# A loop of 200 matmuls without a reader behind the last product of an AdaLoRA linear layer

## Chip, cores and metric

The kernel runs on one core of a Trainium2 chip. The metric is the device time of one execution in microseconds. The kernel before takes 162.21 us (median of 3 runs, 161.91 to 162.54).

## What is computed

A linear layer with a low-rank addition whose rank directions are scaled. There are 16 x 2048 = 32,768 rows of 256 inputs, 256 outputs, and rank 16, all in float32:

```python
x_flat = x.reshape(-1, in_dim)            # 32768 x 256
y = x_flat @ W                            # 256 x 256
lora_out = x_flat @ lora_A                # 256 x 16
lora_out = lora_out * lora_E
lora_out = lora_out @ lora_B              # 16 x 256
y = y + scale * lora_out
```

The input is 33.5 MB and the output the same, so 67 MB pass between HBM and SBUF.

## The kernel before

**Folding.** The low-rank part is folded into the weights once: `weff = W + (lora_A * lora_E * scale) @ lora_B`, in bf16 (L158 to L176). After that the kernel is one product, `x @ weff`.

**Tiling.** The rows are cut into six pieces (`PLAN`: 48, 32, 48, 32, 48, 48 rows for each of the 128 partitions). A piece lives in one of four SBUF slots named `xy`, and its outputs overwrite its inputs there. A piece is worked through in steps of 8 rows per partition (`S = 8`), 32 steps in all (`NS`).

**One step on each engine.**

- VectorE rounds 8 x 256 inputs to bf16 (`rounded`, L151, into `xb`) and later copies the transposed step out of PSUM (`copied`, L155, from `ps_xt` to `xt`).
- TensorE transposes a step with 8 matmuls against the identity (`transposed`, L190; two bf16 travel as one float32 word) and multiplies a step with 16 matmuls (`multiplied`, L201): the weights loaded into the array are a 128x128 slice of `xt`, the moving operand is half of `weff` (128x256), and the result goes to `ps_y`.
- ScalarE copies each half of a product from `ps_y` into the slot (L224).
- SP, the queue of the loads and stores, issues the store of a piece when its last copy is done (L104, called from L236), and the two late loads.

**Order on TensorE.** Its work is a hardware loop of 16 passes (L211), each with two steps, transposing one step ahead: pass by pass `transposed(1)`, `multiplied(0)`, `transposed(0)`, `multiplied(1)`. Double buffers (index `k`, 0 or 1) hold `xb`, `xt` and `ps_xt`. The last `transposed(0)` transposes a step that does not exist, and its result is not read. The loop's control on TensorE's sequencer is an ALU_OP and a COMPARE_BRANCH at the end of each pass, and one MOVE ahead of it.

**Signals.** TensorE raises `s_t` after each transposed step (VectorE waits for it, and SP for two of its issues) and `s_m` after each half product (ScalarE waits for it). ScalarE returns the buffers of `ps_y` over `can_y`. Behind the loop TensorE has only four waits that reset semaphores (L117 three times, L250). At the very end SP waits until every store has landed (L251, L252).

Of the kernel before, what the change touches and what calls it, by code (L numbers as in the profile page):

```python
# [12 lines left out]
HOLD = 14, 1  # L13

ISSUE_LOAD, ISSUE_STORE = {5: 16}, {3: 26}

S, G = 8, 4
P = 128
# [17 lines left out]
def kernel(tc, x, W, lora_A, lora_B, lora_E, scale, out):  # L36
    nc = tc.nc
# [17 lines left out]
    def sbuf(name, shape, dt):  # L55
        return nc.alloc_sbuf_tensor(name, shape, dt).ap()

    def psum(name, shape, dt):
        return nc.alloc_psum_tensor(name, shape, dt).ap()
# [8 lines left out]
    weff = sbuf("weff", [P, KC, M], BF16)  # L68
# [6 lines left out]
    pairs = [t[:, :, :].rearrange("p s t -> p (s t)").bitcast(BF16).rearrange("p (s t c) -> p s t c", s=S, c=KC) for t in xt]  # L75
    ps_xt = [psum(f"psum_xt{k}", [P, S, P], FP32) for k in range(2)]
# [42 lines left out]
    def take(sem):  # L119
        nc.tensor.wait_ge(sem, 1).then_inc(sem, -1)  # L120
# [66 lines left out]
    def transposed(k):  # L187
        nc.tensor.wait_ge(can_t[k], 1)
        for j in range(S):
            done = nc.tensor.transpose(ps_xt[k][:, j, :], words[k][:, j, :], ident)  # L190
            if j == 1:
                done.then_inc(can_t[k], -1)
        done.then_inc(s_t.sem, 1)

    def multiplied(k):
        take(can_m)
        for h in range(S // G):
            nc.tensor.wait_ge(can_y[h][k], 1)
            for j in range(G):
                for c in range(KC):  # L200
                    done = nc.tensor.matmul(  # L201
                        ps_y[h][:, j, :], pairs[k][:, h * G + j, :, c], weff[:, c, :],
                        start=(c == 0), stop=(c == KC - 1))
                if j == 0:
                    done.then_inc(can_y[h][k], -1)
            done.then_inc(s_m.sem, 1)
# [4 lines left out]
    with nc.tensor.Fori(0, NS // 2):  # L211
        for k in range(2):
            transposed(1 - k)
            multiplied(k)
    s_t.total, s_m.total = NS + 1, NS * S // G

    for h in range(S // G):
# [2 lines left out]
    for i, r in [(i, r + g) for i, r in steps for g in range(0, S, G)]:  # L220
        n += 1
        nc.scalar.wait_ge(s_m.sem, n)
        t, h = divmod(n - 1, S // G)
# [64 lines left out]
```

## Time and profile before

| what | value |
|---|---|
| profiled execution, time | 162.07 us |
| its span, first to last instruction | 160.7 us |
| mean granted TensorE clock | 0.829 of full speed |
| TensorE matmuls: busy, share of the span, count | 92.6 us, 58%, 780 |
| TensorE weight loads | 83.6 us, 52%, 780 |
| VectorE | 76.7 us, 48% |
| ScalarE | 63.2 us, 39% |
| moved by DMA | 67.42 MB, mean 419 GB/s |

The span counts from the first to the last instruction; 1.37 us of the execution lie outside it. A matmul's duration runs from its start to the modelled end of its result and overlaps the next matmul's, so a pace is read from starts or from merged pieces, not from a mean duration. In lists of groups, `PEld` is the weight load and `PEldq` or `PEq` the sequencer of TensorE; the `xN` is a count.

### The profile page before, as it was taken

To read this page: it belongs to the slowest core of one execution; us is meant where nothing else is said; L and a number is where in the kernel's file an instruction comes from. 1 tells how busy PE (TensorE), PEld (TensorE's weight loads), DVE (VectorE), ACT (ScalarE), POOL (GpSimd) and SP (SyncE) were. 2 spreads that over 40 slices of the span, in tenths; PEclk is the share of its full clock that TensorE was granted. 3 is DMA by queue.
4 is the path that set the end of the run, shared out by engine and by line. 5 is a ranking of instruction groups with operands and counts; after the bars stand their busy time and mean duration, and the time that the engine had idled before them with its cause. 6 is when DMAs were issued, how large, how long until landed. Compare 5 with 4: busy or idle time off the path is not lost.

```text
span 160.7 us, 1867 instructions
## 1 busy us (share of the span) xinstructions
PE 92.6 (58%) x780; PEld 83.6 (52%) x780; DVE 76.7 (48%) x67; ACT 63.2 (39%) x65; POOL 0.7 (0%) x6
## 2 busy tenths in 40 slices
PE   0258099999999200000299999999999980000000
PEld 0047089999999100000279999999999970000000
DVE  0173396989894000000585989898989510000000
ACT  0303118686777400000026686867777681000000
POOL 0100000000000000000000000000000000000000
PEclk9999959999999965555559999999999999555555
DMA  6999998999999999999999999999999999999994
GB/s 195 420 477 416 400 489 383 446 422 428 432 473 310 504 453 416 400 424 416 501 428 428 404 416 489 428 418 404 428 436 416 432 481 404 428 489 416 428 404 196
DMA packets 2370, 67.42 MB, mean 419 GB/s; under 512 B 432, under 2 KB 448, under 8 KB 576
## 3 DMA queue, kind: packets, MB, share of 16 engines
q1 hardware_dynamic: 2160, 67.37, 98.0%
q10 hardware_dynamic: 208, 0.03, 0.1%
q14 instruction: 2, 0.02, 0.0%
HBM read 33.85 MB, written 33.55 MB: 419 GB/s over the span
## 4 chain that ended last, share of the span: by engine, by line
PE 48%; DMA 30%; ACT 2%; DVE 2%; SPq 1%; issue 0%
PE psum_y L201 31%; DMA out_dram<-xy 20%; PE psum_xt L190 17%; DMA xy<-in_x_dram 11%; ACT xy L224 2%; DVE xb L151 2%; SPq L104 1%
## 5 line engine op out<-in xcount | busy, mean ns | idle before, releaser
L224 ACT COPY xy<-psum_y 128x1024 f32<-128x1024 f32 x64 | 61.9, 1017 | 64.8 <-PE psum_y L201 64.8
L201 PE MATMUL psum_y<-weff,xt 128*128 128x256 bf16 x512 | 63.8, 280 | 0.0
L190 PE MATMUL psum_xt<-ident,xb 128*128 128x128 f32 x264 | 37.6, 291 | 32.3 <-DVE xb L151 32.3
L201 PEld LDWEIGHTS psum_y<-weff,xt 128*128 128x128 bf16 x512 | 51.5, 101 | 6.8
L151 DVE CAST xb<-xy 128x2048 bf16<-128x2048 f32 x32 | 38.9, 1218 | 32.9 <-DMA out_dram<-xy 27.7
L190 PEld LDWEIGHTS psum_xt<-ident,xb 128*128 128x128 f32 x264 | 32.9, 151 | 33.8 <-DVE xb L151 33.4
L155 DVE COPY xt<-psum_xt 128x1024 f32<-128x1024 f32 x32 | 39.2, 1224 | 11.7 <-PE psum_xt L190 11.7
L163 PE MATMUL psum_xt<-ident,a_sb 128*16 128x128 f32 x2 | 0.6, 394 | 5.9 <-POOL ident L137 5.9
L224 ACT ACT_TABLE_LOAD x1 | 1.3, 1283 | 5.2 <-PEq L133 5.2
L163 PEld LDWEIGHTS psum_xt<-ident,a_sb 128*16 128x16 f32 x2 | 0.1, 90 | 5.9 <-issue 5.9
L159 DVE CAST b_bf<-b_sb 16x256 bf16<-16x256 f32 x1 | 0.3, 280 | 5.4 <-DMA b_sb<-in_lora_B_dram 5.4
L172 PE MATMUL psum_xt<-b_bf,ate 16*128 16x256 bf16 x2 | 0.6, 400 | 1.2 <-DVE ate L167 1.2
L167 DVE TENSOR_SCALAR ate<-psum_xt,e_sb 16x256 bf16<-16x256 f32 x1 | 0.5, 472 | 1.6 <-DMA e_sb<-in_lora_E_dram 1.6
L176 DVE TENSOR_TENSOR weff<-w_sb,psum_xt 128x512 bf16<-128x512 f32 x1 | 0.7, 689 | 0.8 <-PE psum_xt L172 0.8
L172 PEld LDWEIGHTS psum_xt<-b_bf,ate 16*128 16x128 bf16 x2 | 0.1, 108 | 1.7 <-DVE ate L167 1.7
L137 POOL TENSOR_SCALAR_AFFINE_SELECT ident<-ident 128x128 f32<-128x128 f32 x1 | 0.3, 298 | 0.2 <-POOL ident L135 0.2
L135 POOL MEMSET ident<- 128x128 f32 x1 | 0.2, 205 | 4.6 <-POOLq L133 4.6
L269 POOL MEMSET const-bfloat16-1.0<- 128x1 bf16 x1 | 0.1, 102 | 0.0
L269 POOL MEMSET const-uint8-127<- 128x1 uint8 x1 | 0.1, 102 | 0.0
L269 POOL MEMSET const-float32-0.0<- 128x1 f32 x1 | 0.1, 99 | 0.2 <-issue 0.2
L269 POOL MEMSET const-float32-1.0<- 128x1 f32 x1 | 0.1, 99 | 0.0
## 6 DMA issues: line engine op xcount, KB each, us to landing
out_dram<-xy SPq DMA_DIRECT2D x4, 6144.0 KB, 29.5
xy<-in_x_dram SPq DMA_DIRECT2D x3, 4096.0 KB, 26.4
xy<-in_x_dram SPq DMA_DIRECT2D x2, 6144.0 KB, 22.6
out_dram<-xy SPq DMA_DIRECT2D x2, 4096.0 KB, 25.4
xy<-in_x_dram SPq DMA_DIRECT2D x2, 3072.0 KB, 36.5
xy<-in_x_dram SPq DMA_DIRECT2D x1, 2048.0 KB, 7.9
w_sb<-in_W_dram SPq DMA_DIRECT2D x1, 256.0 KB, 2.7
a_sb<-in_lora_A_dram ACTq DMA_DIRECT2D x1, 16.0 KB, 2.8
```

Source lines behind the costliest of these rows:

```text
L104: ins = queue.dma_start(**aps)
L137: s_id.by(nc.gpsimd.affine_select(out=ident, in_=ident, compare_op=mybir.AluOpType.not_equal, fill=1.0, base=0, pattern=[[-1, P]], channel ...
L151: nc.vector.tensor_copy(out=xb[t % 2], in_=slot(i)[:, r:r + S, :]).then_inc(can_t[t % 2], 1)
L155: nc.vector.tensor_copy(out=xt[t % 2], in_=ps_xt[t % 2]).then_inc(can_m, 1)
L163: at_done = nc.tensor.transpose(ps_at[:, c, :], a_sb[:, c, :], ident)
L167: s_v.by(nc.vector.tensor_scalar(out=ate, in0=ps_at, scalar1=e_sb, scalar2=float(scale), op0=mybir.AluOpType.mult, op1=mybir.AluOpType.mult))
L172: aeb_done = nc.tensor.matmul(ps_aeb[:, c, :], ate[:, c, :], b_bf, start=True, stop=True)
L176: s_v.by(nc.vector.tensor_add(out=weff, in0=w_sb, in1=ps_aeb))
L190: done = nc.tensor.transpose(ps_xt[k][:, j, :], words[k][:, j, :], ident)
L201: done = nc.tensor.matmul(ps_y[h][:, j, :], pairs[k][:, h * G + j, :, c], weff[:, c, :], start=(c == 0), stop=(c == KC - 1))
L224: y = nc.scalar.copy(out=slot(i)[:, r:r + G, :], in_=ps_y[h])
L269: nc = _bacc.Bacc("TRN2", target_bir_lowering=False, num_devices=1)
```

## The change

One constant, and a second hardware loop on TensorE behind the first. It has 25 passes of 8 matmuls. The weights are slices of `xt1`, the transposed inputs of the last step, and the moving operand is the first half of `weff`. Every matmul writes the same 128x256 float32 part of `ps_xt[0]`, each with `start` and `stop` set, so none adds to another's result. No semaphore is touched, and nothing reads that part again.

```diff
 ISSUE_LOAD, ISSUE_STORE = {5: 16}, {3: 26}
+
+SPARE = 25, 8
...
         for k in range(2):
             transposed(1 - k)
             multiplied(k)
+    with nc.tensor.Fori(0, SPARE[0]):
+        for j in range(SPARE[1]):
+            nc.tensor.matmul(
+                ps_xt[0][:, :2, :].rearrange("p s t -> p (s t)"), pairs[1][:, j, :, 0], weff[:, 0, :],
+                start=True, stop=True)
     s_t.total, s_m.total = NS + 1, NS * S // G
```

## Prediction

> **What bounds the kernel now.** I read the strips of the page first, then the chain of waits in order of time, then stretches of time, then single lines. The strips show 40 slices of 4.02 us each:
>
> ```profile
> PE   0258099999999200000299999999999980000000
> ACT  0303118686777400000026686867777681000000
> PEclk9999959999999965555559999999999999555555
> DMA  6999998999999999999999999999999999999994
> ```
>
> The transfers run at nine tenths or more in nearly every slice. TensorE works in two long blocks, and in the last seven slices (28 us) neither TensorE nor ScalarE does anything: the kernel only drains its last store. The granted TensorE clock falls to half some slices after TensorE goes quiet. So the change puts its work where TensorE is idle and the end is set elsewhere. The end of the chain of waits, in order of time (start us, length us, what), says by what:
>
> ```profile
> 76 pieces in order of time: start us, us, what
> ...
> 127.77 1.75 PE psum_y L201 x16
> 129.51 0.87 PE psum_xt L190 x8
> 130.39 0.89 PE psum_y L201 x8
> 131.27 0.02 issue
> 131.30 0.90 ACT xy L224
> 132.20 0.01 issue
> 132.21 1.02 ACT xy L224
> ```
>
> The last matmuls feed two ScalarE copies that end at 132.21 + 1.02 = 133.23. Behind them SP issues the store of the last piece (48 rows per partition, 6144 KB). The timeline has that issue at 133.25 us, and the span ends at 160.7: the last 27.5 us are that store and what is still queued ahead of it. Stretches of time show the same, and at what rate (columns: us, busy time of each engine, granted clock, DMA share, GB/s):
>
> ```profile
> 20.00:53.00 33.00, 32.93 (x286) 30.28 (x287) 26.98 (x24) 21.73 (x23) 0.00 (x0) 0.95 1.03 434
> 55.00:78.00 23.00, 0.00 (x0) 0.00 (x0) 0.00 (x0) 0.00 (x0) 0.00 (x0) 0.56 0.98 422
> 86.00:131.00 45.00, 45.00 (x415) 41.86 (x414) 37.71 (x32) 32.80 (x34) 0.00 (x0) 1.00 1.00 430
> 133.00:154.00 21.00, 0.00 (x0) 0.00 (x0) 0.00 (x0) 0.22 (x1) 0.00 (x0) 0.58 1.02 440
> ```
>
> With TensorE busy the transfers moved 434 and 430 GB/s, with TensorE idle 422 and 440. Last, the loop control of the existing TensorE loop (L211) and the products (L201), with duration in ns as min/median/max and the first and last start in us:
>
> ```profile
> L211 PEldq ALU_OP  x16: 36/36/42, 21.4 to 130.7; - x16
> L211 PEldq COMPARE_BRANCH  x16: 76/208/217, 21.5 to 130.8; - x16
> L211 PEldq MOVE  x1: 33/33/33, 10.4 to 10.4; - x1
> ```
>
> ```profile
> L201 PEld LDWEIGHTS psum_y<-weff,xt x512: 96/98/152, 13.7 to 131.8; 128*128 128x128 bf16 x171
> L201 PE MATMUL psum_y<-weff,xt x512: 269/273/421, 13.7 to 131.9; 128*128 128x256 bf16 x171
> ```
>
> The sequencer took its last ALU_OP at 130.7 while the last product started at 131.9. It runs 1.2 us, some 11 matmuls, ahead of the array.
>
> **The change, part by part.** It removes nothing, moves nothing, issues no DMA and adds no semaphore wait. It adds one MOVE and 25 passes of 8 weight loads, 8 matmuls, one ALU_OP and one COMPARE_BRANCH, on TensorE's queue alone.
>
> *The array's time.* Each added matmul has the form of L201's: the same weight slice (128x128 bf16 out of xt1), the same moving operand weff, 256 columns. The 273 ns in the row is one matmul from start to finish and overlaps the next, so I take the pace from the chain. Its L201 pieces start at 85.85 and again at 130.39, 17 halves of 24 matmuls later: 44.54 us / 408 = 109 ns. The weight load (98 ns) fits under that, as it does in L201. So 200 x 0.109 = 21.8 us. The first can start one pace behind the last product, at 131.9 + 0.1 = 132.0. The last ends at 132.0 + 199 x 0.109 + 0.27 = 154.0 us.
>
> *The clock.* That pace needs the full grant. It is 1.00 from 86 to 131, and in the stretch after the last product the records drop to half only at 136.4, over 4 us after TensorE fell quiet. The added matmuls come without a gap, so I take 1.00. At half clock the chain has 16 products in 3.41 us (from 81.27), 213 ns each. That is the other end: 200 x 0.213 = 42.6 us.
>
> *Loop control.* A taken branch costs the sequencer about 0.31 us from the start of the ALU_OP to the end of the branch (0.1 + 0.208). One pass gives the array 8 x 0.109 = 0.87 us of work, so the sequencer has 0.56 us left for 16 instructions, 35 ns each. How fast it issues is shown by L201's second half: those 8 products wait for the ScalarE copy that ends at 130.61 (timeline: the pair of copies from 128.68 takes 1.93), and the ALU_OP behind them runs at 130.68. Sixteen instructions went in 0.07 us, 4 ns each. So a pass needs some 0.38 us of sequencer against 0.87 us of array, and branches hide under the matmuls. The existing loop agrees: 45.00 of 45.00 us busy over eight or nine branches. The slow bound comes from the transposes behind a branch: 16 instructions within the 0.70 us from the branch's end (125.75) to the next semaphore instruction (126.45), though that one also waits for VectorE. It gives 0.31 + 0.70 = 1.01 us per pass, 25.3 us in all, end at 157.5. I take 0.87.
>
> *Behind the loop* TensorE has four semaphore instructions (L117 x3, L250), 0.15 us apart in the records. At most 0.6 us, so TensorE is done between 154.0 and 154.6. Nobody waits for it: no later instruction reads ps_xt[0], and the signals that ScalarE and SP need (s_m, s_t) are raised by the old loop.
>
> *Code.* The page has two instruction packets in the whole run (0.02 MB). If the longer program needs one more first-time fetch, the nearest rows are the small loads at the start, 2.8 us (lora_A) and 5.5 us (lora_E) to landing. Even 5.5 moves TensorE's end only to 160.1.
>
> [...]
>
> *The transfers.* The matmuls read SBUF while the last store does. Rates by stretch bound this from both sides: 440 to 430 GB/s would lengthen 21 us by 0.5 us; 422 to 434 would shorten it by 0.6 us. The two idle stretches differ more from each other than from the busy ones, so I take 0.
>
> *Sum.* Profiled execution: span 160.7, time 162.07 (1.37 outside the span). TensorE's new end of 154.0 to 154.6 lies 6.1 to 6.7 us before the span's end, so 162.07 + 0 = 162.1, or, against the median of the runs shown, 162.2. The cover is the last store. Without it, the whole 21.8 us would show.
>
> **Rivals.**
>
> *Slower: the array runs the loop at half clock.* It ends at 132.0 + 42.6 + 0.6 = 175.2, so the time is 176.6. It decides as soon as more than 6.1 / 0.104 = 59 of the 200 matmuls are paced at 213 instead of 109. For it: TensorE would be dense for 69 us (85 to 154), longer than any block in this trace, and grants do change here. Against: both drops come after TensorE went quiet, none inside a block, once granted, for 45 us. 7%.
>
> *Slower: every branch of the new loop stalls for its code.* By the row of the smallest landing, 2.7 us (w_sb), a pass takes 0.31 + 2.7 = 3.0 us, 25 passes 75 us, end at 207.6, time 209. Anything over 0.27 us a pass beyond the 0.87 would show. Against it are the old loop's 15 taken branches without a gap. 3%.
>
> [...]
>
> *Slower: contention.* The matmuls slow the store. By the rates the price is 0.5 us (162.7, within the bound), and beyond 0.5% only if it took twice that, 163.1 or more. 3%.
>
> *Faster.* Only a quicker drain could do it. The rates allow 0.6 us (161.6), again within the bound; beyond that nothing in the profile offers a way, as no work behind 133 us uses TensorE's clock. 5%.
>
> *The change does not do what it says*, the loop being dropped or its matmuls skipped: same time, told from my forecast by the trace alone. 2%, counted with no change.
>
> **How the numbers follow.** About 0.5% (0.8 us) is what a measurement of this kernel can tell from no change. Hidden under the store: 80%, with the dropped loop 82% for same; slower 7 + 3 + 3 = 13%; faster 5%. The likeliest gives 162.2. The range takes the runs' own spread (161.91 to 162.54) and the transfer bounds (-0.6, +0.5, and twice the latter at the upper side): 161.5 to 163.2. What lies outside, 176 and up, is some 10%.
>
> **What would show it.** Right: 200 more matmuls at 109 ns from 132.0 to about 154, clock 1.00 until about 158, the store issued at 133.25 as before, the chain still ending in the store's drain behind ScalarE. Wrong: a chain that ends in TensorE, starts 213 ns apart, gaps every eight matmuls, or less than 430 GB/s between 133 and 154 us.

## The result and the profile after

| | before | changed |
|---|---|---|
| median of 7 runs | 162.21 us (161.91 to 162.54) | 163.22 us (162.95 to 163.88) |
| ratio, 95% interval | | 1.0064 (1.0048 to 1.0081) |
| profiled execution, time | 162.07 us | 163.88 us |
| its span | 160.7 us | 162.5 us |

The changed kernel is slower by 0.64%, some 1.0 us. The profiled execution is the slowest of the seven, so its sums come out higher than the medians. Line numbers are those of the changed kernel: L203 is the product, L219 the new matmul, L106 the store.

The strips of the page of the changed kernel (40 slices of 4.06 us):

```profile
PE   0159099999999400000399999999999999999700
ACT  0301306776868500000046867768686840000000
PEclk9999858999999985555579999999999999999995
DMA  5999998999999999999999999999999999899990
GB/s 168 441 472 411 411 484 381 454 411 448 444 444 351 474 399 399 436 411 524 411 411 399 520 411 399 399 510 423 399 436 403 411 532 399 387 423 508 411 399 36
```

TensorE is now busy into slice 38, and the clock falls only in the last one. There the DMA engines stand at 0 tenths and 36 GB/s, where the kernel before had 4 tenths and 196 GB/s in its last slice: the drain has a thin tail. The group of the new matmuls and the end of the chain of waits:

```profile
L219 PE MATMUL psum_xt<-weff,xt 128*128 128x256 bf16 x200 | 22.0, 273 | 0.0
```

```profile
129.85 1.75 PE psum_y L203 x16
131.59 21.83 PE psum_xt L219 x200
```

The 200 matmuls run at 21.83 / 200 = 109 ns and end at 153.4, nine microseconds before the span does. So the chain that the view prints is not what ended last: it starts from the last instruction that an engine was busy with, and SP's wait for the last store is none. The true end is in the stretches behind the matmuls (columns: us, busy time by engine, granted clock, DMA share, GB/s). First the kernel before, then the changed one:

```profile
159.00:160.00 1.00, 0.00 (x0) 0.00 (x0) 0.00 (x0) 0.00 (x0) 0.00 (x0) 0.50 0.01 0
160.00:161.00 1.00, 0.00 (x0) 0.00 (x0) 0.00 (x0) 0.00 (x0) 0.00 (x0) 0.50 0.00 0
```

```profile
133.00:154.00 21.00, 20.43 (x188) 18.05 (x185) 0.00 (x0) 0.00 (x0) 0.00 (x0) 1.00 1.03 445
...
160.00:161.00 1.00, 0.00 (x0) 0.00 (x0) 0.00 (x0) 0.00 (x0) 0.00 (x0) 0.50 0.11 49
```

While the matmuls ran, the transfers moved 445 GB/s, against 440 without them. The sum did not suffer. But 49 GB/s over 1 us is 49 KB: one single packet (49,152 bytes) on one of the 16 DMA engines. It started at 160.19 us and ran until 162.0, and the other 15 engines were through by 160.5.

The trace keeps every packet and, for each store, the moments at which its 16 parts landed (one for each DMA engine). A packet's record in the kept trace does not name its engine; packets that follow one another without a gap are read here as one engine's, which gives 16 such rows. From those records:

```
first and last of the 16 landings, us     kernel before        changed kernel
store issued 112.1 / 111.6                130.01  131.63       130.22  132.41
store issued 117.5 / 117.0                144.51  146.23       144.69  147.66
last store, 133.3 / 132.7                 158.99  160.71       159.19  162.48

packets of 49,152 bytes of the engine that landed last (start us: took ns), kernel before
109.3: 1905   111.2: 1924   113.2: 1924   115.1: 1909   117.0: 1924   118.9: 1914   ...
131.1: 1912   133.0: 1848   all later ones: 1815 to 1819

the same, changed kernel
...  131.90: 1933   133.83: 1905   135.73: 1905   137.63: 1914   139.54: 1905   141.44: 1895   143.34: 1914
     145.25: 1924   147.17: 1904   149.07: 1905   150.97: 1909   152.88: 1867   154.74: 1815
     156.55: 1815   158.37: 1829   160.19: 1815
the other 15 engines in that time: 1815 each
```

In the kernel before, the last landing trails the first by 1.6 to 1.7 us, through all three stores. In the changed one the distance grows from 2.19 to 2.97 to 3.29 us, by 1.1. One engine's packets took 1.905 us in place of 1.815, 5% more, until the last added matmul had ended; in the kernel before, the engine that landed last is back at 1.815 us from 135 us on. Ten or eleven such packets in a row are behind by 11 x 0.09 = 1.0 us, which is the loss. The other 0.8 us by which the two profiled executions differ was there before the new loop: at 130 us the distance was 2.19 against 1.63, and the first landings were 0.2 later.

### The profile page after: what moved, and what is told of

Its sections match the earlier page's. It is cut to its first block, busy times and chain, and to the rows that moved or that the text cites. A ratio compares the mean times of both kernels' runs of the same rounds, so it can differ in the third digit from the quotient of the medians.

```text
span 162.5 us, 2318 instructions
## 1 busy us (share of the span) xinstructions
PE 115.1 (71%) x980; PEld 103.5 (64%) x980; DVE 76.7 (47%) x67; ACT 63.2 (39%) x65; POOL 0.8 (0%) x6
## 4 chain that ended last, share of the span: by engine, by line
PE 61%; DMA 30%; DVE 2%; ACT 1%; SPq 0%; issue 0%
PE psum_y L203 31%; DMA out_dram<-xy 19%; PE psum_xt L192 16%; PE psum_xt L219 13%; DMA xy<-in_x_dram 11%; DVE xb L153 2%; ACT xy L231 1%; SPq L106 0%
## 5 line engine op out<-in xcount | busy, mean ns | idle before, releaser
L203 PE MATMUL psum_y<-weff,xt 128*128 128x256 bf16 x512 | 64.5, 282 | 0.0
L203 PEld LDWEIGHTS psum_y<-weff,xt 128*128 128x128 bf16 x512 | 51.8, 101 | 7.2
L219 PE MATMUL psum_xt<-weff,xt 128*128 128x256 bf16 x200 | 22.0, 273 | 0.0
L219 PEld LDWEIGHTS psum_xt<-weff,xt 128*128 128x128 bf16 x200 | 19.6, 98 | 2.3
```

What stands on the lines that cost most here:

```text
L203: done = nc.tensor.matmul(ps_y[h][:, j, :], pairs[k][:, h * G + j, :, c], weff[:, c, :], start=(c == 0), stop=(c == KC - 1))
L219: nc.tensor.matmul(ps_xt[0][:, :2, :].rearrange("p s t -> p (s t)"), pairs[1][:, j, :, 0], weff[:, 0, :], start=True, stop=True)
```

## The experiments

Three theories. A: each instruction that leaves a record in the trace costs one DMA engine a little, whatever it does. B: the matmuls' reads of SBUF slow the engine. C: the loop's branches fetch code over it. Each edit is against the changed kernel, if nothing else is said. Time differences are the ratio's share of the median before, with its 95% interval.

### The change again

> The changed kernel once more, as the measure for the others on this chip. Theory A (each TensorE instruction or its record costs one of the 16 DMA engines a little) and theory B (the matmuls' reads of SBUF cost it) both expect about 1.0 us over the kernel before, one engine's 49152-byte packets at 1.90 us in place of 1.815 from the end of the loads to the last matmul, and a spread of the last store's 16 completions of some 3 us against 1.7. The rival that the 1.0 us is chance of the chip expects a ratio of 1.00.

Measured: ratio 1.0058 (1.0035 to 1.0081), +0.9 us (0.6 to 1.3). The slowed packets took 1905 ns (median), and the distance of the 16 landings grew from 1.45 to 2.56 us. It is not chance, and it has the same place.

### Half the instructions for the same array time

```diff
-SPARE = 25, 8
+SPARE = 25, 4
...
-                ps_xt[0][:, :2, :].rearrange("p s t -> p (s t)"), pairs[1][:, j, :, 0], weff[:, 0, :],
+                ps_xt[0][:, :4, :].rearrange("p s t -> p (s t)"), pairs[1][:, j, :, 0],
+                weff[:, :, :].rearrange("p c m -> p (c m)"),
```

> The loop has 100 matmuls of 512 columns in place of 200 of 256: half the instructions over about the same 21.6 us, and the same moving reads per us. Theory A: the slowed packets take about 1.86 us, the price is about 0.5 us. Theory B: 1.90 us and about 1.0 us, as with 200.

Measured: 1.0018 (0.9999 to 1.0037), +0.3 us (0.0 to 0.6). The loop ran until 153.5 us, as long as that of the change, and the slowed packets took 1867 ns: an excess of 52 in place of 90 ns. That speaks for A. B had the same moving reads per us and expected no difference from the change. In the profiled execution the slowed engine was not the last one when the loop began. At the end its part landed 0.3 us later than the next one, so at most that much of its delay reached the time there.

### The same instructions on a quarter of the partitions

```diff
-                ps_xt[0][:, :2, :].rearrange("p s t -> p (s t)"), pairs[1][:, j, :, 0], weff[:, 0, :],
+                ps_xt[0][:, :2, :].rearrange("p s t -> p (s t)"), pairs[1][:32, j, :, 0], weff[:32, 0, :],
```

> The loop's 200 matmuls read 32 of the 128 partitions, weights and moving operand both; the count and the pace of 109 ns stay. Theory A: packets at 1.90 us and about 1.0 us as before. Theory B: a quarter of the reads, packets at 1.815 to 1.84 us, 0 to 0.3 us.

Measured: 1.0609 (1.0576 to 1.0641), +9.9 us. Neither theory expected this: the granted clock fell. Stretches of this kernel and its loop in the chain of waits:

```profile
133.00:136.00 3.00, 3.00 (x29) 2.52 (x28) 0.00 (x0) 0.08 (x1) 0.00 (x0) 0.98 1.14 492
136.00:140.00 4.00, 4.00 (x21) 2.78 (x19) 0.00 (x0) 0.00 (x0) 0.00 (x0) 0.50 0.97 418
```

```profile
131.99 39.01 PE psum_xt L219 x200
```

Some 4 us after the last full product the grant fell to half, though TensorE stayed busy without a gap, and the loop took 39.0 us. It ended at 171.0 us, and with it the span. Here TensorE sets the end, so the time says nothing on A or B, but the packets do. At half clock there were half as many instructions per us (10.5 in place of 21.0), and the slowed packets took 1858 ns, an excess of 43. The reads per us were an eighth of the change's. By B that would leave 11 ns.

### Empty instructions

```diff
-            nc.tensor.matmul(
-                ps_xt[0][:, :2, :].rearrange("p s t -> p (s t)"), pairs[1][:, j, :, 0], weff[:, 0, :],
-                start=True, stop=True)
+            nc.tensor.nop()
```

> The loop holds 200 empty instructions in place of 200 matmuls: nothing is read and the array rests. Theory A: while the loop runs (some 10 to 30 us, its pace is not known) one engine's packets are longer than 1.815 us, by an amount that goes with the number of instructions per us. Theory B: 1.815 us throughout and the time of the kernel before.

Measured: 0.9999 (0.9977 to 1.0020). A pass took 0.36 us. The empty instructions left no record, so only the loop's control stands in the trace, 25 times an ALU_OP and a COMPARE_BRANCH from 130.8 to 139.8 us. In that time one engine's packets took 1829 to 1867 ns, 1836 in the middle: a small excess from the loop's control alone, without a matmul or a weight load. To see if empty instructions are executed at all, 64 were put in a pass in place of 8:

> 25 passes of 64 empty TensorE instructions (8 before). If they are executed, a pass takes longer than the 0.36 us of before, by some 0.4 us at the 7 ns each that the difference to bare loop control suggests. They leave no record in the trace. If it is the instruction that costs the DMA engine, packets are at 2.0 us or more while it runs; if it is the record, they stay at 1.82 to 1.83, from the loop control alone.

Measured, in the one run of it: a pass took 0.36 us again, the slowed packets 1829 to 1848 ns, and the kernel 162.15 us. Eight or 64, they took no time, so they were most likely never executed, and what an instruction without a record costs stays open.

### Fewer passes

```diff
-SPARE = 25, 8
+SPARE = 10, 8
```

> The loop has 10 passes in place of 25: 80 matmuls, 160 array instructions, over at about 140.7 us. Theory A (each recorded instruction costs one DMA engine some 2.4 ns): packets at 1.90 us until about 140.7 us and at 1.815 us behind it, 0.4 us over the kernel before. A loss that comes from having the loop at all (its code, its branches' first fetch) would stay at 1.0 us.

Measured: 1.0018 (0.9997 to 1.0038), +0.3 us (0.0 to 0.6). The packets took some 1.91 us up to the one that started at 138.8, 1867 ns at 140.7, and 1815 to 1834 after. So the packets are slowed as long as the matmuls run. It is not a fixed price of having a loop. How much time 80 matmuls cost is less sure: the interval reaches from nothing to more than the 0.4 us expected. And in the profiled execution they cost none. There another engine landed last, whose packets took 1815 ns all through the loop: the distance of the 16 landings was 2.89 us at 133 us and again at the end. The slowed engine's last packet ended 0.9 us ahead of that one's. The delay of one engine reaches the time only as far as that engine is the last.

### No loop, no branches

```diff
-    with nc.tensor.Fori(0, SPARE[0]):
-        for j in range(SPARE[1]):
-            nc.tensor.matmul(
-                ps_xt[0][:, :2, :].rearrange("p s t -> p (s t)"), pairs[1][:, j, :, 0], weff[:, 0, :],
-                start=True, stop=True)
+    for j in range(SPARE[0] * SPARE[1]):
+        nc.tensor.matmul(
+            ps_xt[0][:, :2, :].rearrange("p s t -> p (s t)"), pairs[1][:, j % S, :, 0], weff[:, 0, :],
+            start=True, stop=True)
```

> The 200 matmuls written out one behind another, no loop, no branch. Theory A: packets at 1.90 us until about 153 us and 1.0 us over the kernel before, as with the loop. The rival that the loop's branches fetch code over that DMA engine: 1.815 us per packet and 0 to 0.3 us; instead some instruction packets of 8 KB more in the list of queues.

Measured: 1.0045 (1.0026 to 1.0063), +0.7 us (0.4 to 1.0). The slowed packets took 1895 ns until 152 us. C falls: without a branch they are slowed as with 25. Nor did the changed kernel fetch code in its loop: its page has two instruction packets, as that of the kernel before, and they lie at 54.9 and 105.8 us. The straight code did bring its own fetches, a second queue of instruction packets on the page:

```profile
q8 instruction: 2, 0.03, 0.1%
q14 instruction: 2, 0.02, 0.0%
```

### Many small matmuls in half the time

```diff
-SPARE = 25, 8
+SPARE = 25, 16
...
-                ps_xt[0][:, :2, :].rearrange("p s t -> p (s t)"), pairs[1][:, j, :, 0], weff[:, 0, :],
+                ps_xt[0][:32, 0, :64], pairs[1][:, j % S, :32, 0], weff[:, 0, :64],
```

> 400 matmuls of 64 columns against 32 columns of weights, in 25 passes of 16: twice the instructions, each reading a quarter of the moving and of the weight columns, at perhaps 30 to 60 ns a pair. Theory A: the slowed packets take longer than 1.90 us while it lasts (2.0 us at 60 ns a pair, 2.2 us at 30) and the price is about 1.9 us, although it is over sooner. Theory B (the price goes with the reads): half the reads of the 200, 0.5 us or less.

Measured: 1.0113 (1.0083 to 1.0142), +1.8 us (1.3 to 2.3). The loop in its chain of waits:

```profile
131.34 11.77 PE psum_xt L219 x400
```

It is over at 143.1 us, ten earlier than the change's, and the kernel loses nearly twice as much. The slowed packets took 2187 ns, 20% more, and 1815 again from 146 us on; the distance of the 16 landings grew from 1.72 to 3.73 us. This is the clearest cut between A and B: half the reads, twice the instructions, about twice the loss.

### Another engine's instructions

The loop is taken out and VectorE gets 300 small copies behind its last step:

```diff
+    idle = sbuf("idle", [P, 300, 8], FP32)
...
     nc.vector.sem_inc(can_t[NS % 2], 1)
+    for j in range(300):
+        nc.vector.tensor_copy(out=idle[:, j, :], in_=ident[:, :8])
```

> No loop on TensorE. VectorE makes 300 copies of 128x8 float32 behind its last step, from 129 us on, at some 60 ns each. Theory A in its wide form (instructions of any engine cost the same DMA engine): packets at about 1.88 us while they last, 0.5 to 0.7 us over the kernel before. In its narrow form (TensorE's alone, or another DMA engine for VectorE's): one engine slowed that was not the last, 0 to 0.4 us, or no longer packets at all and 0.

Measured: 1.0074 (1.0050 to 1.0097), +1.2 us (0.8 to 1.6). One engine's packets took 1876 ns while the copies ran (127.5 to 149.3 us, 73 ns apart), so A holds in its wide form: VectorE's instructions cost an engine as TensorE's do, 2.4 ns each in the table below (whether it is the same engine, the records do not say). It is more than the 0.5 to 0.7 us expected. The straight code also brought three more instruction packets, and two packets of data that met one took 0.4 and 0.5 us longer, and each of these instruction packets took 0.3 us itself; how much of the rest they explain was not separated. In the profiled execution the engine with these two packets and the one slowed by the copies ended level, at 161.26 and 161.25 us.

### Earlier in the kernel

The same 300 copies into the same tile `idle`, put into VectorE's wait for the second store, again without the loop:

```diff
         if t == HOLD[0]:
 
+            for j in range(300):
+                nc.vector.tensor_copy(out=idle[:, j, :], in_=ident[:, :8])
             for _ in range(10):
```

> No loop on TensorE. VectorE's 300 copies of 128x8 lie in its long wait for the second store (about 52 to 78 us), where TensorE rests; first stores alone are moved, from 68 us on loads too. By the per-instruction price of 2.5 ns, one engine's store packets are at about 1.87 us in place of 1.815 from 54 us on while the copies last (some 22 us), and if that holds only while nothing but stores is moved, back at 1.815 from 68 us on. The engine is behind by 0.4 to 0.7 us. If it carries that to the end, since no engine ever rests, 0.3 to 0.7 us over the kernel before; if the lag is made up in the waits between, 0.

Measured: 1.0068 (1.0044 to 1.0093), +1.1 us (0.7 to 1.5). But for their first two microseconds or so, the copies lie where TensorE is idle:

```profile
L152 DVE COPY idle<-ident x300: 158/160/163, 51.2 to 73.2; 128x8 f32<-128x8 f32 x150
```

One engine's 48 KB store packets took about 1.87 us while they ran. The distance of the 16 landings was 0.60 us for the load that landed at 53 us, 2.29 for the store at 79, and still 2.54 at the end (2.54 to 2.59 at every transfer from 93 us on): a lag that arises 80 us ahead of the end is carried there. Again it is more than the price per instruction gives, and again the page has more instruction packets (four in place of two). As for what is moved: the loads and stores of `xy` are in one queue (q1) and land in the order of their issue. In the kernel before, the load issued at 68.4 us has its first packet at 76.4; the second store, issued at 46.7, landed at 77.2 to 78.0. The packets slowed from 68 to 72 us belong to that store. So the point that I had set at 68 us was wrong: the load issued then moves behind that store.

### One price for all

Excess of the slowed engine per us, divided by the recorded instructions of all engines per us in the same stretch:

```
kernel, stretch in us               instructions per us   excess, ns per us   ns per instruction
loop control alone, 132 to 139              6.5                 14.8                 2.3
32 partitions, 136 to 159                  10.5                 25.0                 2.4
512 columns, 135 to 150                    10.6                 28.6                 2.7
VectorE behind, 133 to 147                 13.6                 32.3                 2.4
VectorE early, 56 to 73                    13.7                 31.8                 2.3
no loop, 134 to 150                        18.4                 43.2                 2.3
the change, 133 to 151                     21.0                 48.7                 2.3
the change again, 133 to 151               21.1                 49.9                 2.4
small matmuls, 133 to 141                  73.1                170.6                 2.3
kernel before, stores, 108 to 130          21.2                 55.4                 2.6
kernel before, loads, 86 to 103            20.8     one packet at 0.5%              -
```

(Packets that met an instruction packet are left out.) Over a factor of eleven in rate, whether the instructions are TensorE's or VectorE's and whatever they do in these runs, it is about 2.4 ns an instruction. (The trace of the 512 columns has 75 of its 100 matmuls. Counted with the missing ones, that row has 11.8 instructions per us and gives 2.4 too.) The change records some 445 instructions behind 132 us: 445 x 2.35 = 1.05 us. All of it shows in the time, because the slowed engine was the last one there before the loop as well.

The last two rows show the condition. The kernel before has the same effect in its own last stores (2.6 ns at 21.2 instructions per us), and next to none while loads run at 20.8 (one packet at 0.5%).

What carries the 2.4 ns is not shown. That it is the recording of the instructions is my reading: the price was the same (2.3 to 2.7 ns) for every kind of recorded instruction that was tried. No run here shows an instruction that was executed without a record, and all runs were timed with the recording on, so whether the loss exists without it was not tried.

## Why the prediction was wrong

I forecast 162.2 us, within 161.5 to 163.2, and no change. It is 163.22, just outside, and slower by more than the bound of 0.5%.

- **The array's time: right.** 200 matmuls at 109 ns, ended at 153.4 us (forecast 154.0, from a last product that came half a microsecond earlier in this execution). Clock 1.00 until 158.7 us.
- **Loop control: right.** 24 taken branches of 208 ns each and no gap at the array. The rival that each branch stalls for its code did not happen: that a branch can do so was my assumption, and no run here shows it. Without any branch the packets were slowed all the same (1895 ns).
- **The cover: right, but not as a whole.** TensorE ended nine microseconds ahead of the end, and nobody waited for it.
- **The transfers: the step that failed.** "Rates by stretch bound this from both sides", I wrote, and took 0 in between bounds of -0.6 and +0.5 us. The rates are means over 16 DMA engines, and the mean even rose (445 GB/s). The end is set by the engine that lands last. That one lost 5% for 20 us, which is 0.3% in the mean and 1.0 us at the end. So both the term and its bounds were sized on the wrong quantity.
- **The price could be read from the trace before.** There one engine's 48 KB packets take 1905 to 1924 ns from 107 to 119 us, the 32 KB ones 1274 to 1312 in place of 1213 from 121 to 130 us, and 1815 again as soon as TensorE rests. Eleven packets at +0.09 us, put under the last store, would have given 163.2 for this change. I had the contention rival at 3% and priced it by the mean rate at 0.5 us, with 163.1 us or more at twice that price. The time came out there, but the rate that was to show it did not fall.
- **The rival of the half clock** did not happen here (7% given). The run on 32 partitions shows what it does: the loop ended at 171.0 us and the time was 172.5. My price of 176.6 put the whole loop at half clock, but the first 4 us still had the full one. I had counted two drops of the clock in the kernel before; its trace has three (at 20.3, 57.8 and 136.4 us), and all three come after TensorE went quiet, so that argument stands.
- **What would show it:** I had named a chain that ends in TensorE as a sign of a wrong forecast. It does end there in the view, and TensorE still did not set the end. That sign was ill chosen. So was the sign of less than 430 GB/s: the rate was 445.

## What to carry to other kernels

Where a kernel ends in the drain of one big transfer, look at the landings of its 16 parts, not at GB/s: here the slowest DMA engine set the end (162.48 us, the first landing at 159.19), and 0.3% in the mean was 1.0 us there. Work that was "free" because its engine idled still paid for its instructions in this measurement: some 2.4 ns each on one DMA engine while stores ran, and as much of it in the time as that engine was behind all others (with 80 matmuls it ended 0.9 us ahead of the last one, and cost none in the profiled execution). The same array work in half as many instructions slowed its packets by 52 ns in place of 90. When weighing a cover, ask what the hidden work does to the thing that covers it.

## Not expected of the hardware

- Matmuls on 32 of 128 partitions, back to back, lost the granted clock 4 us after the last full product (at 135.9 us) and ran at half for 35 us. The small matmuls (128 partitions, 32 columns of weights, 64 moving) kept it over their 11.8 us: it fell at 148.3 us, 5 us after they had ended.
- A pair of weight load and matmul of that small form went at 11.77 us / 400 = 29 ns.
